# All engines issue in the written order, the softmax goes behind the rope, the cut one slot later

## The chip, the cores and the metric

The kernel runs on one core of a Trainium2 chip. Its time is the device time of one execution in microseconds (us), given as the median of several runs. The core's engines are TensorE (PE in the rows; its weight loads are PEld), VectorE (DVE), ScalarE (ACT), GpSimd (POOL) and SyncE (SP), which issues most of the DMAs. Each engine takes its instructions strictly in order: one that waits holds up all that stands behind it on that engine.

## What is computed

Two layers of a decoder over all 512 positions of one sequence, in float32. Both have 16 heads of 128, four key and value heads, and a gate beside the attention:

```
def dsa_mixer(h, w_in, q_g, k_g, w_out):
    q, k, v, gate, qi, ki, wi = split_cols(h @ w_in, A_WIDTHS)
    q = rope(rms_norm(q.reshape(B, T, N_HEADS, HEAD_DIM), q_g), pos)
    k = rope(rms_norm(k.reshape(B, T, N_KV_HEADS, HEAD_DIM), k_g), pos)
    ...
    logits = jnp.where(valid, jnp.einsum('bqgrd,bqkgd->bqgrk', qb, k_sel) * scale, NEG)
    p = jax.nn.softmax(logits, axis=-1)
    o = jnp.einsum('bqgrk,bqkgd->bqgrd', p, v_sel)
    return (jax.nn.silu(gate) * o) @ w_out

def moba_mixer(h, w_in, q_g, k_g, w_out):
    ...

h = h + dsa_mixer(rms_norm(h, a_norm[0]), ...)
h = h + moba_mixer(rms_norm(h, b_norm[0]), ...)
```

In the first layer an indexer keeps the 128 best keys of each query (the part left out in the middle); the second layer is the same without an indexer, with causal attention over blocks of 256 keys.

## The kernel before, in words

**Slots.** All projections are cut into tiles of 128 output columns over 2048 input rows, and each tile into four quarters. A quarter is a slot: `units` lists 484 of them in the order in which TensorE takes them. A weight quarter is loaded as `raw`, split two slots ahead into a high and a low part (`split`: `whi` cast on ACT, `wlo` subtracted on DVE), and multiplied in twelve 512-column matmuls, high by high, high by low and low by high (`products`, L193 to L195). The first 36 slots belong to layer 0's indexer. Then each layer has four groups of 40 slots: a k tile, a v tile, and four heads' q and gate tiles in the order q0 q1 g0 q2 g1 q3 g2 g3. Layer 0's output tiles begin at slot 196, layer 1 at 260, its output tiles at 420.

**A loop over slots** (the end of `build`) writes, for slot i: the split of slot i + 2, raw loads, the twelve matmuls, `maybe_attend`, and then the functions that were hung on this slot with `later(k, f)`, in the order in which they were hung; `later(k, f, True)` puts one at the front.

**A q tile** whose last slot is D hangs up s1 on D + 1 (square and its first bf16 part b0 on ACT, then the rope: four operations on DVE), s2 on D + 2 (the other two bf16 parts: sq minus b0 on DVE, b1 on ACT, b2 on DVE; then qh on ACT and ql on DVE) and the column sums on D + 3 (`sums`, cs, twelve small matmuls on TensorE that need b0, b1 and b2; one slot later for the first eight heads of layer 0). A k tile goes alike.

**A head's attention** begins with twelve score matmuls at a slot A (`attend`, L444 to L446) and hangs up the rest: `soft` on A + 1 (four masked maxima and four biases nb on DVE, four exponentials on ACT), `norm` on A + 2 (a reciprocal on DVE, four scalings on ACT), `turn` on A + 2 (four block transposes of 128x320 on DVE into u), `move` on A + 3 and A + 4 (16 DMAs from u to pt, which SP issues), `cuts` on A + 7 (pt is split into ph, cast on ACT, and pl, subtracted on DVE), `pv` on A + 9 (15 matmuls with the values on TensorE), and `gate` and `rest` on A + 10 and A + 11. Attends stand at least seven or eight slots apart (`maybe_attend`). In layer 1 they come at offsets 15, 23, 31 and 39 of a group's 40 slots (30 and 37 for the last two heads), so that `soft` of a group's first, second and third head falls into a slot that also holds the s1 of a q tile.

**What sets the order.** PE and SP issue in the written order throughout (`manual_schedule`, L106). ACT, DVE and POOL do so only for the first 46 slots (`OPENING`); behind them the framework's scheduler orders these three when the program is built. The orders in the section on the change show what it chose.

The lines of the call order:

```
for i in range(len(units)):
    ...
    split(i + SPLIT)
    ...
    load(i + SPLIT)
    ...
    products(i)
    maybe_attend(A if i < second else B)
    pending = hooks.get(i, [])
    while pending:
        pending.pop(0)()
```

Of the kernel before, what the change touches and what calls it, by code (L numbers as in the profile page):

```python
# [93 lines left out]
def build(tc, a):  # L94
    nc = tc.nc
    ctx = ExitStack()
# [6 lines left out]
    dp = pool("dram", space=DRAM)  # L103
    pp = pool("psum", space=PSUM)
    E = mybir.EngineType
    ctx.enter_context(tc.manual_schedule(engines={E.PE, E.SP}))  # L106
    opening = ExitStack()
    opening.enter_context(tc.manual_schedule(engines={E.Activation, E.DVE, E.Pool}))

    def t512(tag, name, dt=F32, bufs=None, p=None, cols=T):  # L110
        return (p or kp).tile([P, cols], dt, tag=tag, name=name, **({"bufs": bufs} if bufs else {}))
# [22 lines left out]
    def later(k, f, first=False):  # L134
        fs = hooks.setdefault(now[0] + k, [])
        fs.insert(0 if first else len(fs), f)
# [1 line left out]
    def at(slot, f):  # L138
        hooks.setdefault(slot, []).append(f)

    OPENING = 46
    SLOT, SPARE = 2.6, 0.5
    dve, gps = Paced(nc.vector, 1.05e-3), Paced(nc.gpsimd, 2.1e-3)

# [15 lines left out]
    def load(upto, most=99):  # L160

        while most and issued[0] < len(loads) and (issued[0] < RAW or loads[issued[0] - RAW][3] <= upto):
            t, q, m, _ = loads[issued[0]]
            raw = wp.tile([P, 4 * m, t.cols], F32, tag="raw", name=f"raw_{t.name}_{q}", bufs=RAW)
            src = t.src.rearrange("p (k n) -> p k n", n=t.cols)
            nc.sync.dma_start(raw, src[:, 4 * q:4 * (q + m)])
            for k in range(m):
                t.raw[q + k] = raw[:, 4 * k:4 * k + 4]
            issued[0] += 1
            most -= 1  # L170

    def split(i):
        if i >= len(units):
            return
        t, q = units[i]
        hi = wp.tile([P, 4, t.cols], F32R, tag="whi", name=f"whi_{t.name}_{q}", bufs=3)
        lo = wp.tile([P, 4, t.cols], F32R, tag="wlo", name=f"wlo_{t.name}_{q}", bufs=3)
        r = t.raw[q]
        nc.scalar.copy(hi, r)  # L179
        eng = gps if fill else dve  # L180
        eng.tensor_tensor(lo, r, hi.bitcast(F32), op=OP.subtract)
        t.cut[q] = (hi, lo)

    def products(i):
        t, q = units[i]
        if q == 0:
            t.z = ps("pj", f"z_{t.name}", 3)
        hi, lo = t.cut[q]
        o = t.z[:t.cols, :T - t.t0]
        for k in range(4):  # L190
            kt = 4 * q + k
            xh, xl = (x[:, t.t0:] for x in t.X[kt])
            nc.tensor.matmul(o, lhsT=hi[:, k], rhs=xh, start=kt == 0, stop=False)  # L193
            nc.tensor.matmul(o, lhsT=hi[:, k], rhs=xl, start=False, stop=False)  # L194
            nc.tensor.matmul(o, lhsT=lo[:, k], rhs=xh, start=False, stop=kt == KT - 1)  # L195
        if q == 3:
            t.done(t.z)
# [33 lines left out]
    def cut_hi(hi, src):  # L231
        nc.scalar.copy(hi, src)

    def cut_lo(lo, src, hi):
        dve.tensor_tensor(lo, src, hi.bitcast(F32), op=OP.subtract)
# [198 lines left out]
    def attend(Y, h):  # L434
# [43 lines left out]
        def move(js):  # L478
            for j in js:
                for i in range(4):  # L480
                    nc.sync.dma_start(v.t[BLK * j:BLK * j + BLK, 320 * i:320 * i + 320],  # L481
                                      v.u[BLK * i:BLK * i + BLK, 320 * j:320 * j + 320])

        def cuts(hi, lo):
            if 0 in hi:
                v.ph = t512("ph", f"ph{n}", F32R, cols=1280)
                v.pl = t512("pl", f"pl{n}", F32R, cols=1280)
            for i in hi:
                o = slice(640 * i, 640 * i + 640)
                cut_hi(v.ph[:, o], v.t[:, o])  # L490
            for i in lo:
                o = slice(640 * i, 640 * i + 640)
                cut_lo(v.pl[:, o], v.t[:, o], v.ph[:, o])
# [25 lines left out]
        def rest():  # L519
            cut_lo(Y.B[h][1], v.og, Y.B[h][0])  # L520

        later(1, soft, True)
        for k, f in ((2, norm), (2, turn), (3, lambda: move((0, 1))), (4, lambda: move((2, 3))),
                     (7, lambda: cuts((0, 1), (0, 1))), (9, pv), (10, gate), (11, rest)):
            later(k, f)

    def maybe_attend(Y):
        h = Y.head
        apart = 7 if h >= HEADS - 2 or (Y.L == 0 and h < 12) else 8
        if h < HEADS and Y.open and h in Y.qslot and now[0] >= Y.qslot[h] + 4 and now[0] >= Y.slot + apart:  # L530
            Y.head, Y.slot = h + 1, now[0]
            attend(Y, h)
# [258 lines left out]
    def load_x(q):  # L791
        for kt in range(4 * q, 4 * q + 4):
            nc.sync.dma_start(xs[kt], a["xT"][kt])

    def take_x(q):
        for kt in range(4 * q, 4 * q + 4):
            take(X0, kt, xs[kt], gains[:, kt:kt + 1], 0)
# [16 lines left out]
    split(1)  # L814
    for i in range(len(units)):
        now[0] = i
        if i == OPENING:
            opening.close()
        dve.slot(i * SLOT)
        gps.slot(i * SLOT)  # L820
        if i in (2, 4):
            take_x(i // 2 + 1)
        split(i + SPLIT)
        if i == 0:
            take_x(1)
        if i in (0, 1):
            load(i + SPLIT, 1)
            load_x(i + 2)
        load(i + SPLIT)
        if i == 1:  # L830
            for n, t in (("cosi", cosi), ("sini", sini), ("cos", cos), ("sin", sin)):
                nc.sync.dma_start(t, a[n])
# [5 lines that stand above are left out]
        while fill and dve.until < (i + 1) * SLOT - SPARE:  # L838
            fill.pop(0)()
# [56 lines left out]
```

## Time and profile before

| | |
|---|---|
| median of 3 runs | 1519.15 us (1518.68 to 1520.04) |
| profiled execution | 1520.94 us |
| its span in the profile | 1519.2 us |
| mean granted clock of TensorE | 0.991 |
| DVE busy | 912.1 us, 60% |
| ACT busy | 695.2 us, 46% |
| POOL busy | 146.6 us, 10% |
| DMA | 170.86 MB, 112 GB/s mean |

The profile is that of one execution, which took 1.8 us more than the median. The span runs from its first to its last instruction. Busy times are sums over the span; matmuls are pipelined, so that one of 512 columns is shown with 0.39 us though the next starts some 0.23 us behind it. Names of tiles are given without their numbers: `cs_q` is any q tile's column sums. L77 is the line of a helper through which most operations of DVE and POOL are written, so these are told apart by their tiles. What stands in square brackets behind a row is the engine's idle time just before it, and what ended it.

### The profile page before, as it was taken

The numbers are of one execution on the slowest core, as the hardware profiler recorded it, in microseconds if no ns is written. First come the engines' busy times: TensorE is split into PE (matmuls) and PEld (weight loads), VectorE is DVE, ScalarE is ACT, GpSimd is POOL, SyncE is SP. The second block draws the span as 40 slices with busy tenths as digits, with TensorE's granted clock in tenths as the row PEclk, the third lists the DMA queues.
The fourth block names the chain that finished last, engine by engine and source line by source line (L and its number), as shares of the span: only waits on it lengthen the run. The fifth ranks groups of instructions, "written<-read, shape, count | busy, mean of one in ns | idle before, by whom it ended". The sixth has DMA issues, their size and how long they took to land.

```text
span 1519.2 us, 20709 instructions
## 1 busy us (share of the span) xinstructions
PE 1488.3 (98%) x7348; PEld 1244.3 (82%) x7348; DVE 912.1 (60%) x1848; ACT 695.2 (46%) x1332; POOL 146.6 (10%) x128
## 2 busy tenths in 40 slices
PE   8999999999899999899999999999999999899999
PEld 6998888888787888788888888887888888788887
DVE  6898966666666665644344565667565657543322
ACT  6874334545454444533333444455444545432221
POOL 0433540000000000001111000000000000000000
PEclk9999999999999999999999999999999999999999
DMA  7332223333323323254443233332323332344442
GB/s 246 105 97 84 86 95 103 102 106 100 108 83 112 107 74 116 76 172 146 146 145 125 80 97 113 102 100 91 115 87 118 100 113 88 90 126 163 146 145 90
DMA packets 74215, 170.86 MB, mean 112 GB/s; under 512 B 13824, under 2 KB 30976, under 8 KB 74112
## 3 DMA queue, kind: packets, MB, share of 16 engines
q1 hardware_dynamic: 74112, 169.55, 35.4%
q8 instruction: 57, 0.93, 0.2%
q14 instruction: 46, 0.38, 0.1%
HBM read 140.13 MB, written 8.39 MB: 98 GB/s over the span
## 4 chain that ended last, share of the span: by engine, by line
PE 64%; DVE 4%; SPq 3%; ACT 2%; issue 2%; DMA 1%; DVEq 0%; ACTq 0%
PE z_o L193 8%; PE z_o L194 8%; PE z_o L195 8%; PE z_g L193 5%; PE z_q L193 5%; PE z_q L195 5%; PE z_q L194 5%; PE z_g L195 4%; PE z_g L194 4%; SPq L481 3%; PE o L508 2%; PE z_v L193 1%; PE z_v L195 1%; PE z_v L194 1%; PE z_k L193 1%
## 5 line engine op out<-in xcount | busy, mean ns | idle before, releaser
L193 PE MATMUL z_g<-xh,whi_g 128*128 128x512 f32 x512 | 206.6, 403 | 0.0
L195 PE MATMUL z_g<-xh,wlo_g 128*128 128x512 f32 x512 | 203.1, 397 | 3.2 <-DVE wlo_g L77 3.2
L193 PE MATMUL z_q<-xh,whi_q 128*128 128x512 f32 x512 | 202.6, 396 | 0.0
L194 PE MATMUL z_g<-xl,whi_g 128*128 128x512 f32 x512 | 202.5, 395 | 0.0
L195 PE MATMUL z_q<-xh,wlo_q 128*128 128x512 f32 x512 | 200.1, 391 | 0.0
L194 PE MATMUL z_q<-xl,whi_q 128*128 128x512 f32 x512 | 199.8, 390 | 0.0
L193 PE MATMUL z_o<-bh,whi_o 128*128 128x512 f32 x512 | 199.6, 390 | 0.0
L195 PE MATMUL z_o<-bh,wlo_o 128*128 128x512 f32 x512 | 199.4, 390 | 0.0
L194 PE MATMUL z_o<-bl,whi_o 128*128 128x512 f32 x512 | 199.4, 389 | 0.0
L77 DVE TENSOR_TENSOR wlo_o<-raw_o,whi_o 128x512 fp32r<-128x512 f32 x128 | 88.9, 694 | 159.8 <-ACT whi_o L179 159.8
L179 ACT CAST whi_o<-raw_o 128x512 fp32r<-128x512 f32 x128 | 79.7, 622 | 220.0 <-PE z_o L194 211.5
L179 ACT CAST whi_g<-raw_g 128x512 fp32r<-128x512 f32 x128 | 78.0, 616 | 113.6 <-PE z_q L194 73.6
L179 ACT CAST whi_q<-raw_q 128x512 fp32r<-128x512 f32 x128 | 78.6, 618 | 107.8 <-PE z_q L194 59.9
L195 PEld LDWEIGHTS z_g<-xh,wlo_g 128*128 128x128 f32 x512 | 97.9, 191 | 26.0 <-DVE wlo_g L77 4.5
L77 DVE TENSOR_TENSOR wlo_g<-raw_g,whi_g 128x512 fp32r<-128x512 f32 x112 | 76.5, 686 | 68.3 <-ACT whi_g L179 66.1
L193 PEld LDWEIGHTS z_g<-xh,whi_g 128*128 128x128 f32 x512 | 97.9, 191 | 19.6 <-ACT whi_g L179 1.1
L194 PEld LDWEIGHTS z_g<-xl,whi_g 128*128 128x128 f32 x512 | 98.2, 192 | 18.8
L195 PEld LDWEIGHTS z_q<-xh,wlo_q 128*128 128x128 f32 x512 | 96.2, 188 | 20.5
L195 PEld LDWEIGHTS z_o<-bh,wlo_o 128*128 128x128 f32 x512 | 96.2, 188 | 20.0
L193 PEld LDWEIGHTS z_o<-bh,whi_o 128*128 128x128 f32 x512 | 96.1, 188 | 19.9
L194 PEld LDWEIGHTS z_q<-xl,whi_q 128*128 128x128 f32 x512 | 96.6, 189 | 19.2
L194 PEld LDWEIGHTS z_o<-bl,whi_o 128*128 128x128 f32 x512 | 96.2, 188 | 19.6
(167 smaller groups left out, 2707.3 us busy)
## 6 DMA issues: line engine op xcount, KB each, us to landing
pt<-u SPq DMA_DIRECT2D x512, 40.0 KB, 1.9
raw_q<-w_a SPq DMA_DIRECT2D x32, 512.0 KB, 3.8
raw_g<-w_a SPq DMA_DIRECT2D x32, 512.0 KB, 3.9
raw_q<-w_b SPq DMA_DIRECT2D x32, 512.0 KB, 3.6
raw_g<-w_b SPq DMA_DIRECT2D x32, 512.0 KB, 3.8
raw_o<-w_ao SPq DMA_DIRECT2D x26, 512.0 KB, 3.5
raw_o<-w_bo SPq DMA_DIRECT2D x26, 512.0 KB, 3.6
raw_qi<-w_a SPq DMA_DIRECT2D x14, 512.0 KB, 3.9
```

What stands on the lines that cost most here:

```text
L77: return f(out, *args, **kw)
L179: nc.scalar.copy(hi, r)
L193: nc.tensor.matmul(o, lhsT=hi[:, k], rhs=xh, start=kt == 0, stop=False)
L194: nc.tensor.matmul(o, lhsT=hi[:, k], rhs=xl, start=False, stop=False)
L195: nc.tensor.matmul(o, lhsT=lo[:, k], rhs=xh, start=False, stop=kt == KT - 1)
L481: nc.sync.dma_start(v.t[BLK * j:BLK * j + BLK, 320 * i:320 * i + 320], v.u[BLK * i:BLK * i + BLK, 320 * j:320 * j + 320])
L508: nc.tensor.matmul(o[:, q], lhsT=l[:, kt * P:kt * P + P], rhs=r[:, t], start=m == 0 and c == 0, stop=m == 4 and c == 2)
```

## The change

`manual_schedule` now takes in all five engines for the whole program, and the 46-slot opening is dropped. `soft` is no longer put at the front of its slot's functions but behind those already there. `cuts` stands eight slots behind the scores, no longer seven.

```
-    ctx.enter_context(tc.manual_schedule(engines={E.PE, E.SP}))
-    opening = ExitStack()
-    opening.enter_context(tc.manual_schedule(engines={E.Activation, E.DVE, E.Pool}))
+    ctx.enter_context(tc.manual_schedule(engines={E.PE, E.SP, E.Activation, E.DVE, E.Pool}))
...
-    OPENING = 46
...
-        later(1, soft, True)
+        later(1, soft)
         for k, f in ((2, norm), (2, turn), (3, lambda: move((0, 1))), (4, lambda: move((2, 3))),
-                     (7, lambda: cuts((0, 1), (0, 1))), (9, pv), (10, gate), (11, rest)):
+                     (8, lambda: cuts((0, 1), (0, 1))), (9, pv), (10, gate), (11, rest)):
             later(k, f)
...
-        if i == OPENING:
-            opening.close()
```

The order of PE and of SP is the same, instruction for instruction. On POOL three operations of layer 1's causal mask move. ACT and DVE change in many places; three follow. A name such as `wlo_g1_4_2` is the low weights of layer 1, gate tile of head 4, quarter 2; `S1_4` and `nb1_4` are head 4's scores and bias; ISA rows are the masked maximum and the reading of its accumulator.

DVE in layer 1, the slot that holds head 4's `soft` and the rope of head 5's q tile. Before:

```order
L77 TENSOR_TENSOR wlo_g1_4_2_9477<-raw_g1_4_2_9342,whi_g1_4_2_9476 128x512
L77 ISA S1_4_9493,mx1_4_9495<-s0_1_4_9457,mask_93 128x512
L77 ISA mx1_4_9495 128x1
L77 SCALAR_TENSOR_TENSOR t1_q1_5_9515<-z_q1_5_9360,gains_79,cos_91 128x512
L77 SCALAR_TENSOR_TENSOR nb1_4_9496<-mx1_4_9495,sc_q1_4_9474 128x1
L77 ISA S1_4_9493,mx1_4_9495<-s1_1_4_9458,mask_93 128x384
```

and after:

```order
L77 TENSOR_TENSOR wlo_g1_4_2_9474<-raw_g1_4_2_9339,whi_g1_4_2_9473 128x512
L77 SCALAR_TENSOR_TENSOR t1_q1_5_9496<-z_q1_5_9357,gains_77,cos_89 128x512
L77 SCALAR_TENSOR_TENSOR t2_q1_5_9497<-z_q1_5_9357,gains_77,sin_90 64x512 x2
L77 TENSOR_TENSOR t1_q1_5_9496<-t1_q1_5_9496,t2_q1_5_9497 128x512
L77 ISA S1_4_9502,mx1_4_9504<-s0_1_4_9454,mask_91 128x512
L77 ISA mx1_4_9504 128x1
L77 SCALAR_TENSOR_TENSOR nb1_4_9505<-mx1_4_9504,sc_q1_4_9471 128x1
```

Before, the first maximum stood right behind the weights, the rope's four operations were spread between and behind the maxima. Now the whole rope stands in front of the first maximum.

DVE a dozen rows on, the slot with the second and third bf16 part of head 5's q tile and with the transposes of head 4. Before:

```order
L77 TENSOR_TENSOR sq_q1_5_9509<-sq_q1_5_9509,b0_q1_5_9511 128x512
L77 TENSOR_TENSOR t1_q1_5_9515<-t1_q1_5_9515,t2_q1_5_9516 128x512
L77 TENSOR_TENSOR wlo_g1_4_3_9522<-raw_g1_4_2_9342,whi_g1_4_3_9521 128x512
L77 TENSOR_TENSOR b2_q1_5_9513<-sq_q1_5_9509,b1_q1_5_9512 128x512
L77 TENSOR_TENSOR ql_q1_5_9543<-t1_q1_5_9515,qh_q1_5_9542 128x512
L77 RECIPROCAL ri1_4_9546<-sm1_4_9494 128x4
L77 TENSOR_TENSOR wlo_q1_6_0_9559<-raw_q1_6_0_9389,whi_q1_6_0_9558 128x512
L77 STREAM_TRANSPOSE u1_4_9552<-S1_4_9493 128x320 x4
```

and after:

```order
L77 TENSOR_TENSOR wlo_g1_4_3_9519<-raw_g1_4_2_9339,whi_g1_4_3_9518 128x512
L77 TENSOR_TENSOR sq_q1_5_9490<-sq_q1_5_9490,b0_q1_5_9492 128x512
L77 TENSOR_TENSOR b2_q1_5_9494<-sq_q1_5_9490,b1_q1_5_9493 128x512
L77 TENSOR_TENSOR ql_q1_5_9540<-t1_q1_5_9496,qh_q1_5_9539 128x512
L77 RECIPROCAL ri1_4_9543<-sm1_4_9503 128x4
L77 STREAM_TRANSPOSE u1_4_9549<-S1_4_9502 128x320 x4
L77 TENSOR_TENSOR wlo_q1_6_0_9556<-raw_q1_6_0_9386,whi_q1_6_0_9555 128x512
```

The weights wlo_q1_6_0 stood ahead of the four transposes and now stand behind them.

ACT in layer 0, the cast ph of head 5. Before:

```order
L179 CAST whi_k0_2_3_3809<-raw_k0_2_2_3616 128x512
L232 CAST ph0_5_3842<-pt0_5_3707 128x640 x2
L179 CAST whi_v0_2_0_3850<-raw_v0_2_0_3716 128x512
L460 ACTIVATE S0_6_3866,sm0_6_3867<-S0_6_3866,nb0_6_3869,sc_q0_6_3411 128x512
L460 ACTIVATE S0_6_3866,sm0_6_3867<-S0_6_3866,nb0_6_3869,sc_q0_6_3411 128x384
```

and after:

```order
L176 CAST whi_k0_2_3_3806<-raw_k0_2_2_3607 128x512
L176 CAST whi_v0_2_0_3841<-raw_v0_2_0_3713 128x512
L229 CAST ph0_5_3857<-pt0_5_3704 128x640 x2
L457 ACTIVATE S0_6_3863,sm0_6_3864<-S0_6_3863,nb0_6_3866,sc_q0_6_3392 128x512
L457 ACTIVATE S0_6_3863,sm0_6_3864<-S0_6_3863,nb0_6_3866,sc_q0_6_3392 128x384
```

Here ph moves one row down, behind the next slot's high weights. In layer 1 it stands between whi_g1_5_1 and whi_g1_5_2 (head 4) in both orders, so it doesn't move there.

## Rows read from the trace of the kernel before

**Rows 1.** The page's part 1: engine, busy us, share of the span, instructions.

```profile
PE 1488.3 (98%) x7348; PEld 1244.3 (82%) x7348; DVE 912.1 (60%) x1848; ACT 695.2 (46%) x1332; POOL 146.6 (10%) x128
```

**Rows 2.** Waits of TensorE over the whole span: us in total, times, longest us.

```profile
PE cs_q L298 <- ACT b_q L291: 9.5, 3, 3.7
PE cs_k L298 <- DVE b_k L77: 4.3, 1, 4.3
PE z_g L195 <- DVE wlo_g L77: 3.2, 3, 1.1
PE cs_q L298 <- DVE b_q L77: 3.1, 5, 1.0
```

**Rows 3.** Windows, the stretches behind the four big stalls: us, busy (x), PEclk, DMA share, GB/s.

```profile
1318.66:1325.05 6.39, 6.39 (x24) 5.06 (x25) 1.81 (x4) 0.62 (x1) 1.01 (x1) 0.50 0.26 63
sum 23.14, PE 22.95 PEld 18.27 DVE 6.07 ACT 1.84 POOL 4.34; mean PE 5.74 PEld 4.57 DVE 1.52 ACT 0.46 POOL 1.08
```

**Rows 4.** Waits of all engines: us in total, times, longest us.

```profile
ACT ph L232 <- DMA pt<-u: 90.1, 29, 5.9
```

**Rows 5.** Timeline of DVE, layer 1 from head 4's softmax: start us, us.

```profile
994.02 0.69 DVE L77 TENSOR_TENSOR wlo_g<-raw_g,whi_g 128x512 fp32r<-128x512 f32 x1 [2.52 <-ACT whi_g L179]
...
999.01 0.69 DVE L77 TENSOR_TENSOR sq_q<-sq_q,b_q 128x512 f32<-128x512 f32 x1
...
1000.82 0.69 DVE L77 TENSOR_TENSOR b_q<-sq_q,b_q 128x512 bf16<-128x512 f32 x1
...
1002.12 0.66 DVE L77 TENSOR_TENSOR wlo_q<-raw_q,whi_q 128x512 fp32r<-128x512 f32 x1
1004.24 1.69 DVE L77 STREAM_TRANSPOSE u<-S 128x320 f32<-128x320 f32 x4 [1.47 <-ACT S L467]
```

**Rows 6.** Timeline of DVE, a rope (layer 1) and a first maximum (layer 0).

```profile
853.53 0.75 DVE L77 SCALAR_TENSOR_TENSOR t_q<-z_q,gains,cos 128x512 f32<-128x512 f32 x1
854.29 1.52 DVE L77 SCALAR_TENSOR_TENSOR t_q<-z_q,gains,sin 64x512 f32<-64x512 f32 x2
...
368.46 0.68 DVE L77 CUSTOM_DVE_ANT_0 S<-s,mask 128x512 f32<-128x512 f32 x1
...
369.25 0.16 DVE L77 SCALAR_TENSOR_TENSOR nb<-mx,sc_q 128x1 f32<-128x1 f32 x1
```

**Rows 7.** Timeline of ACT, the same heads as rows 5.

```profile
996.09 0.82 ACT L460 ACTIVATE S<-S,nb,sc_q 128x512 f32<-128x512 f32 x1 [0.95 <-DVE nb L77]
...
998.84 0.60 ACT L179 CAST whi_g<-raw_g 128x512 fp32r<-128x512 f32 x1
...
1002.29 1.92 ACT L467 ACTIVATE S<-S,ri 128x512 f32<-128x512 f32 x4 [0.81 <-DVE ri L77]
```

**Rows 8.** Timeline of TensorE: sums, next tile's first matmul, two attends (layer 1).

```profile
1003.47 0.45 PE L298 MATMUL cs_q<-ones_bf,b_q 128*128 128x1 bf16 x12
...
1006.64 0.39 PE L193 MATMUL z_q<-xh,whi_q 128*128 128x512 f32 x1
...
1017.53 0.39 PE L444 MATMUL s<-kh_k,qh_q 128*128 128x512 f32 x1
...
1043.68 0.39 PE L444 MATMUL s<-kh_k,qh_q 128*128 128x512 f32 x1
```

**Rows 9.** Timelines of ACT and DVE, the loop from ph to ph (layer 1).

```profile
1018.65 1.36 ACT L232 CAST ph<-pt 128x640 fp32r<-128x640 f32 x2 [3.25 <-DMA pt<-u]
...
1019.41 1.56 DVE L77 TENSOR_TENSOR pl<-pt,ph 128x640 fp32r<-128x640 f32 x2 [3.29 <-ACT ph L232]
...
1031.57 1.69 DVE L77 STREAM_TRANSPOSE u<-S 128x320 f32<-128x320 f32 x4 [0.87 <-ACT S L467]
...
1045.88 1.36 ACT L232 CAST ph<-pt 128x640 fp32r<-128x640 f32 x2 [4.34 <-DMA pt<-u]
```

**Rows 10.** Timelines of ACT and DVE, layer 0, between heads 13 and 14.

```profile
605.52 1.36 ACT L232 CAST ph<-pt 128x640 fp32r<-128x640 f32 x2 [3.99 <-DMA pt<-u]
...
620.01 0.68 DVE L77 TENSOR_TENSOR b_q<-sq_q,b_q 128x512 bf16<-128x512 f32 x1
```

## The prediction

> **What bounds the kernel now.** I began with the page's busy times: TensorE is busy 1488.3 us of the 1519.2 [rows 1]. [...]
>
> The waits of TensorE come next [rows 2]. The column sums of a rotary tile (cs, L298) wait for its second bf16 part b1 (ACT, L291), 9.5 us in three waits, once for k's third part (4.3) and five times for q's b2 (3.1). That is 16.9 at four places: k's, and three where a wait for b1 (the longest 3.7, so 2.9 each for the other two) is followed by one of up to 1.0 for b2. Three slots of gates wait for their low weights (z_g on wlo_g), 3.2 us. Behind each of the four big stalls the granted clock falls to 0.50, for 23.14 us in sum [rows 3]; at half speed that costs 11.6. So the stalls that can be given back are worth 16.9 + 11.6 + 3.2 = 31.7 us of 1521.
>
> Then the waits of the other engines [rows 4]: ACT stands 90.1 us in 29 waits at ph, the first cast of a head's probabilities, waiting for the transfers of pt. Those transfers feed back on themselves. ACT and DVE go in order, so what stands behind ph and pl (the next head's softmax, then the transposes that start the next transfers) is late when ph is late. From head 5's ph to head 6's ph are 1045.88 − 1018.65 = 27.2 us [rows 9], while TensorE needs 1043.68 − 1017.53 = 26.15 from attend to attend [rows 8]. The loop is a little longer than TensorE's period, so heads drift later until a longer interval between attends lets them catch up.
>
> **The change part by part.** *The cut one slot later* costs nothing where the transfers are late anyway. In layer 1 ph already stood one row behind the next slot's high weights, and stays there (the sentence behind the third pair of orders). In layer 0 it falls behind one more 0.6 us cast, which ACT's wait of up to 5.9 at that place covers; without that cover it is 0.6 us on the loop.
>
> *The softmax behind the rope.* Before, the scheduler wove a head's four masked maxima through the rope of a later q tile. Now the rope goes first, then the maxima with each bias right behind its own. A rope is 0.76 + 1.55 + 0.60 = 2.9 us of DVE, and the first maximum with its bias 0.95 [rows 6]. The exponentials on ACT need all 2.75 us behind that first bias [rows 7], and on ACT the next weights and b1 stand behind them. Before, sums had 2.0 us to spare at a group's first head; 2.9 us more is not covered.
>
> *The transposes ahead of the next weights.* Before, wlo_q6_0 ran at 1002.12 while DVE waited for ACT's normalization; now the four transposes (1004.24 to 1005.93) stand in front of it [rows 5].
>
> First head of a group, from the row of wlo_g at 994.02 [rows 5]. DVE's 512-column operations start 0.60 apart (three from 999.01 to 1000.82). wlo to 994.6, rope to 997.5, first bias 998.45, exponentials to 1001.2, high weights 1001.8, wlo 1002.4, the subtraction of b0 1003.0, b1 1003.7, b2 1004.4. The sums come due at 1003.47 [rows 8]: **1.0 us** of stall. Then ql and the reciprocal to 1005.2, normalization 1.92 [rows 7] to 1007.1, transposes to 1008.8, wlo_q6_0 1009.5. The third matmul needs it at 1006.64 + 0.45 + the 1.0 of slip = 1008.1 [rows 8]: **1.4**. Sum 2.4.
>
> Second and third head, counted from ph. pl is done at 2.2 (0.76 after ph, two of 0.74) [rows 9], wlo 2.8, rope 5.7, first bias 6.7, exponentials 9.4, high weights 9.9, wlo 10.5, the gate's product 11.1, subtraction 11.8, b1 12.5, b2 13.2. ph of head 5 moves with the transposes, from 1018.65 by 2.9 to 1021.6; the sums come due one period after the others, 1003.47 + 26.15, plus 2.4, at 1032.0, that is 10.4 behind ph. Stall **2.9**. Then ql and reciprocal 13.9, normalization 15.9, transposes 17.5, wlo behind them: **1.4** again, 4.3 per head. From the transposes' end (1031.57 + 1.69) to ph are 1045.88 − 1033.26 = 12.6 [rows 9]: the loop becomes 30.1, against a period of 26.15. The two agree: TensorE slips 4.0 to 4.3 per head whether it stands still or runs at the lower clock, because what it loses in one way shortens the next wait. Hence I add no half clock here.
>
> Fourth head: 0.5 (the longer interval absorbs most). Head 14 comes seven slots behind 13 and its softmax had no rope ahead in either order; b2 came 15.2 behind ph (605.52 to 620.69) [rows 10], the late transposes make it 17.3. The stall goes from 3.7 + 1.0 to about 6.8, with 1.5 of half clock (half of the 3 us lost behind a stall now, since a longer wait is followed by less work that is due): 8.3, for 6.9 now (4.7 and 2.2).
>
> Layer 1: three groups of 2.4 + 4.3 + 4.3 + 0.5 = 11.5 are 34.5, the last 2.4 + 4.3 + 8.3 = 15.0, together 49.5. Before it had 3.2 at z_g, 0.4 at one cs, and 2.9 + 1.0 with 3.2 of half clock (half of 6.39) at head 14: 10.7. **+38.8.**
>
> Layer 0: heads 0 to 7 go at intervals of seven slots whose softmax mostly has no rope beside it, and there the plain order is better: heads 0 to 5 no longer drift as far as the longest wait at ph (5.9) [rows 4], and k2's stall of 4.3 with 3.0 of half clock becomes about 1.6. Against that, by the same chains: head 8 2.1 and head 12 2.4 as first heads, head 13 4.4 as a second one, head 14 8.3 and head 9 (cramped like it) 8.1. With k2 that is 26.9. Before, k2 had 7.3, head 9 6.6 (one of the 2.9 stalls with what followed it and its half clock) and head 14 6.9: 20.8. **+6.1.**
>
> Output tiles, the transition between the layers and the index part keep their order but for three mask operations on GpSimd, and have neither softmax nor transposes; I cost them at nothing. Sum: 1520.94 + 38.8 + 6.1 = 1565.8 for a profiled execution, which stands 1.8 above the median of the runs. **1564 us.**
>
> [...] In the rows a 512-column fp32 subtraction is 0.69 us long, yet the next starts 0.60 behind it [rows 5]. [...]
>
> **The rivals.** *Faster, 1488.* The feedback through ph breaks: if ph never waits in front of work that is due, the four stalls go with their half clock, −16.9 − 11.6 − 3.2 from 1520.94, less the 1.8: about 1488. For it: 90.1 us of ACT's time is spent waiting at ph. Against: ph keeps its row in layer 1, and the rope adds 2.9 to the loop. It decides if the loop from ph to ph comes below 26.15. [...]
>
> *No change, 1519.* Layer 0's gain at k2 (about 5.8) and others like it at head 14 balance the losses at the ropes; it needs the softmax to move by under 0.5 us instead of 2.9, as if the weave before had cost nearly what the rope does.
>
> *Slower still, 1590.* The 2.9 us stalls bring the lower clock as those of 2.9 before did [rows 2, 3], some 3 us each in eight places, and the slip doesn't give it back: +24. Against it stands the loop's 30.1.
>
> **How the numbers follow.** Slower by these chains 0.87 (of it 0.12 for the case near 1590), faster 0.09, no change 0.04. What a measurement of this kernel can tell from no change is about 0.2%, 3 us. The bounds come from the chain's error: 1.5 us less in each of 17 stages (bias and exponentials wholly beside the rope) is −25, about 1539; half clock behind each 2.9 us stall about 1590. Range **1536 to 1592**.
>
> **What the changed profile would show.** In layer 1 TensorE's waits for b1 and b2 at L298's place in all four groups (about 1 us at a group's first head, 3 at the second and third), waits of z_q for wlo_q of about 1.4 that the profile before doesn't have; transposes about 3 us later behind attend; the loop from ph to ph near 30 us; the stall at k2 near 1.6. If the loop is 27 or less, my chains are wrong; if the waits at ph vanish and no sums wait, the faster rival holds; if many more than four stretches show 0.50, the slowest does.

## The result and the profile after

The changed kernel takes 1588.86 us (median of 4 runs, 1587.28 to 1589.68) and the kernel before, run beside it, 1519.6: a ratio of 1.045 (95% interval 1.0432 to 1.0468), so 69 us slower. The forecast was 1564, in a range of 1536 to 1592.

The page of the changed kernel begins thus (span, then busy time, share and instructions of each engine):

```profile
span 1585.2 us, 20726 instructions
...
PE 1512.3 (95%) x7348; PEld 1254.9 (79%) x7348; DVE 934.6 (59%) x1848; ACT 689.7 (44%) x1332; POOL 145.8 (9%) x128
```

Against [rows 1] the span grew by 66.0 us. TensorE's idle time grew from 30.9 to 72.9, that is by 42.0, and its busy time by 24.0 for the same 7348 matmuls. The waits of TensorE, with totals, times and longest, say where it stands:

```profile
PE cs_q L295 <- ACT b_q L288: 32.5, 13, 5.5
PE cs_q L295 <- DVE b_q L77: 10.2, 19, 0.6
PE z_q L192 <- DVE wlo_q L77: 7.5, 8, 1.1
PE cs_k L295 <- ACT b_k L288: 4.6, 1, 4.6
PE tv_v L352 <- DVE t_k L77: 3.0, 1, 3.0
```

The sums wait for b1 in 13 places instead of 3, and for b2 in 19 instead of 5 [rows 2]; z_q's waits for low weights behind the transposes are new, eight of them at about 1 us. Twelve times the granted clock falls from 1.00 to 0.50 (half clock below), each time at a wait of TensorE of 1.2 to 5.5 us or just behind it. At 0.50 the 512-column matmuls of a slot start 0.43 us apart (eleven of z_v from 393.59 to 397.86), at 1.00 0.23 (263.02 to 263.92). The first two of these stretches and the sum (us; busy of PE, PEld, DVE, ACT, POOL; granted clock, DMA share, GB/s):

```profile
258.69:262.10 3.41, 3.07 (x10) 2.59 (x11) 2.20 (x5) 2.04 (x4) 0.00 (x0) 0.50 0.76 204
391.81:398.64 6.83, 6.09 (x24) 4.84 (x25) 1.97 (x4) 1.68 (x4) 1.01 (x1) 0.50 0.58 170
...
sum 58.02, PE 49.29 PEld 39.39 DVE 30.63 ACT 29.05 POOL 5.03; mean PE 4.11 PEld 3.28 DVE 2.55 ACT 2.42 POOL 0.42
```

Some begin within the stall, so the busy time in them is what compares: 49.3 us of PE at 0.50, 22.95 in the four of [rows 3]. By the two distances nearly half of the difference is lost by it, which I estimate at 13 us; the other 11 of the 24 I have not assigned.

The slot of head 4 in layer 1, on DVE. It answers to [rows 5]; wlo_g of the first row is the same instruction as the one at 994.02 there:

```profile
1030.61 0.69 DVE L77 TENSOR_TENSOR wlo_g<-raw_g,whi_g 128x512 fp32r<-128x512 f32 x1 [2.46 <-ACT whi_g L176]
1031.22 0.75 DVE L77 SCALAR_TENSOR_TENSOR t_q<-z_q,gains,cos 128x512 f32<-128x512 f32 x1
...
1034.14 0.68 DVE L77 CUSTOM_DVE_ANT_0 S<-s,mask 128x512 f32<-128x512 f32 x1
...
1038.34 0.69 DVE L77 TENSOR_TENSOR wlo_g<-raw_g,whi_g 128x512 fp32r<-128x512 f32 x1 [1.62 <-ACT whi_g L176]
1038.95 0.68 DVE L77 TENSOR_TENSOR sq_q<-sq_q,b_q 128x512 f32<-128x512 f32 x1
1040.32 0.69 DVE L77 TENSOR_TENSOR b_q<-sq_q,b_q 128x512 bf16<-128x512 f32 x1 [0.69 <-ACT b_q L288]
...
1041.53 0.17 DVE L77 RECIPROCAL ri<-sm 128x4 f32<-128x4 f32 x1
1043.75 1.69 DVE L77 STREAM_TRANSPOSE u<-S 128x320 f32<-128x320 f32 x4 [2.05 <-ACT S L464]
1045.37 1.25 DVE L77 TENSOR_TENSOR wlo_q<-raw_q,whi_q 128x512 fp32r<-128x512 f32 x2
```

The square brackets tell the story. DVE stands idle for 1.62 us for the next slot's high weights, then for 0.69 for b1, then for 2.05 for ACT's normalization. Behind the first of these waits stands sq minus b0, whose operands ACT had finished at 1031.73; it runs at 1038.95. The transposes end 14.8 us behind wlo_g, before it was 11.9 (994.02 to 1005.93).

The loop from head 4's ph to head 5's, and two attends of TensorE, answer to [rows 8, 9]:

```profile
1058.02 0.73 ACT L229 CAST ph<-pt 128x640 fp32r<-128x640 f32 x1 [3.46 <-DMA pt<-u]
...
1088.99 0.73 ACT L229 CAST ph<-pt 128x640 fp32r<-128x640 f32 x1 [4.18 <-DMA pt<-u]
...
1056.64 0.39 PE L441 MATMUL s<-kh_k,qh_q 128*128 128x512 f32 x1
...
1086.89 0.39 PE L441 MATMUL s<-kh_k,qh_q 128*128 128x512 f32 x1
```

The loop is 31.0 us (27.2 before) and TensorE's interval between the attends of heads 5 and 6, which answers to it, 30.25 (26.15 before). It slips by 4.1. (The prediction takes the casts at 1018.65 and 1045.88 for those of heads 5 and 6; they are those of heads 4 and 5. Its sums aren't touched by that.)

Stretch by stretch, from the timelines of TensorE (the first score matmul of each head), in us, with two kernels of the experiments beside (man_act and man_sq_ri):

| stretch | before | after | DVE and POOL scheduled | two operations moved |
|---|---|---|---|---|
| start to layer 0's first attend | 221.7 | 222.1 | 220.3 | 219.7 |
| layer 0, head 0 to head 8 | 195.0 | 204.8 | 188.2 | 191.9 |
| layer 0, head 8, to layer 1, head 0 | 446.9 | 463.0 | 449.1 | 452.2 |
| layer 1, head 0 to head 15 | 466.5 | 504.6 | 473.5 | 486.7 |
| layer 1, head 15, to the end | 189.1 | 190.7 | 190.0 | 189.1 |

### The profile page after: what moved, and what is told of

Read it like the earlier page. It is cut to its first block, busy times and chain, and to the rows that moved or that the text cites. A ratio compares the mean times of both kernels' runs of the same rounds, so it can differ in the third digit from the quotient of the medians.

```text
span 1585.2 us, 20726 instructions
## 1 busy us (share of the span) xinstructions
PE 1512.3 (95%) x7348; PEld 1254.9 (79%) x7348; DVE 934.6 (59%) x1848; ACT 689.7 (44%) x1332; POOL 145.8 (9%) x128
## 4 chain that ended last, share of the span: by engine, by line
PE 61%; DVE 13%; ACT 9%; SPq 8%; DMA 4%; issue 4%; POOL 0%; DVEq 0%; ACTq 0%; POOLq 0%
SPq L478 8%; PE z_o L190 7%; PE z_o L191 7%; PE z_o L192 7%; PE z_q L190 4%; PE z_q L191 4%; PE z_q L192 4%; ACT S L457 4%; PE z_g L190 4%; DVE t_q L77 3%; PE z_g L192 3%; PE z_g L191 3%; DMA pt<-u 2%; PE o L505 2%; DVE wlo_g L77 2%
## 5 line engine op out<-in xcount | busy, mean ns | idle before, releaser
L77 DVE TENSOR_TENSOR wlo_o<-raw_o,whi_o 128x512 fp32r<-128x512 f32 x128 | 98.6, 772 | 196.1 <-ACT whi_o L176 196.0
L190 PE MATMUL z_g<-xh,whi_g 128*128 128x512 f32 x512 | 210.8, 412 | 1.4 <-ACT whi_g L176 1.4
L192 PE MATMUL z_g<-xh,wlo_g 128*128 128x512 f32 x512 | 206.7, 404 | 1.6 <-DVE wlo_g L77 1.6
L191 PE MATMUL z_g<-xl,whi_g 128*128 128x512 f32 x512 | 206.3, 403 | 0.0
L77 DVE TENSOR_TENSOR wlo_q<-raw_q,whi_q 128x512 fp32r<-128x512 f32 x114 | 77.1, 684 | 79.6 <-ACT whi_q L176 77.0
L192 PEld LDWEIGHTS z_q<-xh,wlo_q 128*128 128x128 f32 x512 | 96.4, 188 | 32.3 <-DVE wlo_q L77 11.9
L457 ACT ACTIVATE S<-S,nb,sc_q 128x512 f32<-128x512 f32 (+3 forms) x128 | 82.3, 644 | 78.8 <-DVE nb L77 78.8
L190 PEld LDWEIGHTS z_q<-xh,whi_q 128*128 128x128 f32 x512 | 96.9, 189 | 21.1 <-ACT whi_q L176 2.7
```

The lines of the kernel that those rows point to most:

```text
L77: return f(out, *args, **kw)
L457: nc.scalar.activation(s, s, AF.Exp, bias=nb[:, c], scale=sc[:, c], accum_out=v.sm[:, c])
```

## The experiments

Twelve kernels were run. They first took the change apart by its three edits, then by engine, then by operation. Two theories stood at the beginning. Theory A: the loss comes from where the softmax and the cut are written. Theory B: it comes from giving up the scheduler's order, wherever these stand.

### The written order alone (man_only)

```
-        later(1, soft)
+        later(1, soft, True)
...
-                     (8, lambda: cuts((0, 1), (0, 1))), (9, pv), (10, gate), (11, rest)):
+                     (7, lambda: cuts((0, 1), (0, 1))), (9, pv), (10, gate), (11, rest)):
```

> The changed kernel with the softmax back at the front of its slot and the cut back at seven slots, so that the written order of ACT, DVE and POOL alone is left of the change. Theory A (the loss comes from where the softmax, the transposes and the cut are written): layer 1 loses about 1 us at a group's first head (weights behind the transposes) and 2 to 2.5 at the second and third, layer 0 about nothing; 1535 us, between 1525 and 1545. Theory B (the loss comes from giving up the scheduler's weave as such, wherever the softmax is written): most of the 69 us stay, 1570 us or more.

Measured: 1594.28 us, ratio 1.0479 (1.0464 to 1.0495). Theory A falls as it stands: with softmax and cut back in their places the whole loss stays. The rows of the same slot say why the softmax in front doesn't help (DVE, then ACT):

```profile
1037.60 0.75 DVE L77 SCALAR_TENSOR_TENSOR t_q<-z_q,gains,cos 128x512 f32<-128x512 f32 x1 [1.59 <-ACT sq_q L274]
```

```profile
1036.41 0.59 ACT L457 ACTIVATE S<-S,nb,sc_q 128x256 f32<-128x256 f32 x1
...
1036.99 0.58 ACT L274 ACTIVATE sq_q<-z_q 128x512 f32<-128x512 f32 x1
```

Written in front, the softmax takes the square of the q tile behind its exponentials on ACT, and the rope begins 0.03 us behind the square's end. Before, the two were apart: the square and b0 stood ahead of the exponentials on ACT while the maxima stood ahead of the rope on DVE. No order of whole functions gives that, since each function writes on several engines at once. So this kernel takes one delay away and puts another in, and doesn't say what the softmax's place is worth by itself (man_weave below does).

### The cut back at seven slots (man_soft)

```
-                     (8, lambda: cuts((0, 1), (0, 1))), (9, pv), (10, gate), (11, rest)):
+                     (7, lambda: cuts((0, 1), (0, 1))), (9, pv), (10, gate), (11, rest)):
```

> The changed kernel with the cut back at seven slots; the softmax stays behind the rope, the order stays the written one. Theory A with the later cut as the cause of layer 0's loss in heads 0 to 7: those heads win back 10 to 15 us and layer 1 stays within 3 us, 1573 us. The prediction's own step (the later cut costs nothing): within 3 us of 1588.

Measured: 1598.52 us, ratio 1.051 (1.0494 to 1.0526). Both expectations missed. In the written order the later cut doesn't cost, it gives back 9.7 us. ACT's waits at ph are 134.2 us in this kernel:

```profile
ACT ph L229 <- DMA pt<-u: 134.2, 30, 6.8
```

With the cut at eight they are 67.2, so what stands behind ph on ACT is held less at that place. Which of these operations makes the gain was not tested. Layer 1 takes 514.4 us from head 0 to head 15 here and 504.6 with the later cut.

### The softmax in front again, where a rope shares its slot (man_cut8)

```
-        later(1, soft)
+        later(1, soft, 12 <= h < HEADS - 2 or (Y.L == 1 and h < 12))
```

> The changed kernel with the softmax back at the front of its slot in layer 1's heads 0 to 13 and layer 0's heads 12 and 13, the places where a rope shares its slot and attends stand eight slots apart; the cut stays at eight. Theory A (the rope in front of the softmax makes layer 1's loop from ph to ph 30 us): the loop in layer 1 falls to 27.5 to 28.5, layer 1 wins back 15 to 20 us, 1570 us. Theory B: within 5 us of 1588.

Measured: 1586.78 us, ratio 1.0429 (1.0411 to 1.0446), overlapping with the changed kernel's interval. Moved as a whole, the softmax is worth 2 us at most; the loop in layer 1 stays at 31 us (30.8).

### The later cut in the scheduled kernel (sched_cut8)

```
-                     (7, lambda: cuts((0, 1), (0, 1))), (9, pv), (10, gate), (11, rest)):
+                     (8, lambda: cuts((0, 1), (0, 1))), (9, pv), (10, gate), (11, rest)):
```

> The kernel before with the cut at eight slots; the scheduler stays, the softmax stays in front. If the later cut costs by itself, as layer 0 of the changed kernel suggests (ph no longer waits for its transfers and begins up to 5 us behind their landing): 1525 to 1535. If the scheduler moves the cut back to where its data are (in layer 1 it already stood at the later place): within 3 us of 1519.

Measured: 1522.16 us, ratio 1.0009 (1.0000 to 1.0019). The scheduler puts ph where it had stood, or nearly: ACT's waits there are 96.8 us, 90.1 before, and the longest is 5.9 in both. The edit is worth nothing there.

### One engine at a time (man_dve, man_act)

man_dve keeps the written order on DVE alone (beside PE and SP), man_act on ACT alone:

```
-    ctx.enter_context(tc.manual_schedule(engines={E.PE, E.SP, E.Activation, E.DVE, E.Pool}))
+    ctx.enter_context(tc.manual_schedule(engines={E.PE, E.SP, E.DVE}))
```

```
-    ctx.enter_context(tc.manual_schedule(engines={E.PE, E.SP, E.Activation, E.DVE, E.Pool}))
+    ctx.enter_context(tc.manual_schedule(engines={E.PE, E.SP, E.Activation}))
```

> The changed kernel with ACT and POOL given back to the scheduler; DVE stays in the written order. The kernels with the softmax put back in front have shown that its place is not what costs; theory B says that it is the weave given up, and asks on which engine. If it is DVE's order (the rope, the maxima, the transposes ahead of weights that are ready): within 10 us of 1588. If it is ACT's: under 1550.

> The changed kernel with DVE and POOL given back to the scheduler; ACT stays in the written order. If DVE's order costs: under 1550. If ACT's order costs (exponentials ahead of b1, normalization behind qh): within 10 us of 1588.

Measured: man_dve 1565.14 us, 1.0299 (1.0281 to 1.0316); man_act 1524.62 us, 1.003 (1.0019 to 1.0041). It is DVE's order above all: given back to the scheduler together with POOL, it takes 64 of the 69 us with it, though softmax, cut and ACT stay as the change wrote them. (POOL alone was not tried; the change moves three of its operations.) ACT and POOL given back are worth 24 us, and 33 behind the opening, since that kernel's scheduled opening is itself slower by 9.4 (231.5 us to the first attend). The two sum to more than 69, so a part of the loss needs both orders. DVE's rows of man_act, the same slot, and at the end one of the next head's:

```profile
990.67 0.74 DVE L77 SCALAR_TENSOR_TENSOR t_q<-z_q,gains,cos 128x512 f32<-128x512 f32 x1
...
992.97 0.69 DVE L77 CUSTOM_DVE_ANT_0 S<-s,mask 128x512 f32<-128x512 f32 x1
...
995.44 0.69 DVE L77 TENSOR_TENSOR sq_q<-sq_q,b_q 128x512 f32<-128x512 f32 x1
996.04 0.15 DVE L77 SCALAR_TENSOR_TENSOR nb<-mx,sc_q 128x1 f32<-128x1 f32 x1
997.08 0.18 DVE L77 RECIPROCAL ri<-sm 128x4 f32<-128x4 f32 x1 [0.89 <-ACT S L457]
997.59 0.69 DVE L77 TENSOR_TENSOR wlo_g<-raw_g,whi_g 128x512 fp32r<-128x512 f32 x1 [0.33 <-ACT whi_g L176]
998.20 0.68 DVE L77 TENSOR_TENSOR b_q<-sq_q,b_q 128x512 bf16<-128x512 f32 x1
...
1000.45 1.69 DVE L77 STREAM_TRANSPOSE u<-S 128x320 f32<-128x320 f32 x4 [0.29 <-ACT S L464]
...
1022.97 0.69 DVE L77 SCALAR_TENSOR_TENSOR og<-o,gu_g 128x512 f32<-128x512 f32 x1
```

Even here most of the rope stands ahead of the maxima, so with the rest of DVE's order as it is here that costs little. Two other things are different from the changed kernel's rows: sq minus b0 runs among the biases, ahead of the wait for the weights, and the reciprocal stands ahead of the weights and b2. DVE's waits in this stretch are 0.89, 0.33 and 0.29 (and one of 0.52 at u_q) where they were 1.62, 0.69 and 2.05.

### Square, softmax, rope by hand (man_weave)

The kernel with the written order alone, and s1 cut in two, so that a slot's functions are square and b0, softmax, rope:

```
         def s1():
-            v.n = Norm(v.z, n)
             v.r = rope(v.z, Y.qg, n)
+        def s0():
+            v.n = Norm(v.z, n)
...
+            later(1, s0, True)
...
-        later(1, soft, True)
+        put_soft(soft)
...
```

`put_soft` hangs the softmax behind the s0 of its slot and ahead of all else.

> All engines in the written order, cut at seven slots, and in a slot that holds both the order is now square and b0, then the softmax, then the rope, so that neither the rope waits for the exponentials (through the square) nor the maxima for the rope. From the rows: b2 of a group's first head comes just in time, the loop from ph to ph is 28.4 us, 2.2 us of slip at the second and third head of layer 1. If that pair of waits is what the written order costs: 1570 us (1562 to 1578). If it is ready work held behind waits everywhere (weights behind transposes, a v tile behind them): within 6 us of the 1594 that the softmax in front of the square gave.

Measured: 1571.28 us, ratio 1.0334 (1.0319 to 1.035), as worked out from the rows in total, but partly by luck: the loop from head 4's ph to head 5's is 29.2 us, not 28.4, and TensorE slips 3.6 between heads 5 and 6, not 2.2. The coupling through the square was worth 23 of man_only's 74 us. Against man_soft, where the softmax stands behind square and rope and the cut is at seven too, this kernel gains 27 us. So the rope in front of the softmax does cost, where the square is not pushed back for it. (The s0 goes to the front of its slot for every q tile, also ahead of other functions; that part was not taken apart.)

### The sums one slot later (sums4)

```
-            for k, f in ((1, s1), (2, s2), (3 + early, s2b), (4 + early, s3)):
+            for k, f in ((1, s1), (2, s2), (4 if h % GROUP else 3 + early, s2b), (5 if h % GROUP else 4 + early, s3)):
```

> The changed kernel with the column sums of heads 1 to 3 of each group one slot (2.7 us) later, where TensorE now waits for b1 and b2. If the wait at the sums is itself the loss: first and second heads lose nothing there, third heads about 4 us, 1562 us. If TensorE slips because the loop from ph to ph is longer than its period, wherever it waits: the stall shows up elsewhere and the time stays within 6 us of 1588.

Measured: 1582.3 us, ratio 1.0407 (1.0387 to 1.0427), at the edge of the second expectation. The waits at q's sums (32.5 and 10.2) are gone from the list, and others have grown in their place:

```profile
PE z_q L190 <- ACT whi_q L176: 13.2, 11, 2.8
PE z_q L192 <- DVE wlo_q L77: 11.9, 13, 1.1
PE z_g L192 <- DVE wlo_g L77: 10.2, 11, 1.7
PE o L505 <- ACT ph L229: 5.7, 2, 3.1
...
PE z_g L190 <- ACT whi_g L176: 4.2, 4, 1.5
```

These lines hold 45.2 us, in the changed kernel the same five hold 12.2: 33 of the 43 us have moved to the weights and the values. TensorE follows the loop from ph to ph, not the place where it happens to wait.

### Two operations moved by hand (man_sq, man_sq_ri)

In man_sq the first operation of `middle` stands at the end of slot D + 1; in man_sq_ri the reciprocal of `norm` also stands at the end of its softmax's slot. Everything else is the changed kernel, all engines in the written order. `end` hangs a function behind all others of a slot:

```
+            end(1, lambda: v.n.first())
             for k, f in ((1, s1), (2, s2), (3 + early, s2b), (4 + early, s3)):
...
         later(1, soft)
+        end(1, recip)
```

> The changed kernel, all engines in the written order, with one operation per rotary tile moved by hand to where the scheduler had put it: sq minus b0 stands at the end of slot D + 1, ahead of the next slot's low weights instead of behind them (with its engine it waits there for the high weights, which stand behind the exponentials). If the loss is ready work queued behind that wait: b1, b2 and the transposes come 1.4 us earlier, the slip at the second and third head of layer 1 falls from 4.1 to 2.7, 1568 us. If the place of the weights and transposes is what costs: within 6 us of 1588.

> As the kernel with sq minus b0 moved, and the reciprocal of the softmax also moved up, to the end of its softmax's slot, so that ACT's normalization no longer waits behind b2 and ql of DVE. By the rows 0.8 us earlier transposes on top: slip 1.9 per head, 1558 us. If the reciprocal's place is of no account: within 4 us of the kernel with sq alone.

Measured: man_sq 1572.05 us, 1.0342 (1.0326 to 1.0358); man_sq_ri 1542.69 us, 1.0146 (1.0133 to 1.016). One 0.6 us operation per tile moved by one place is worth 17 us, one of 0.17 us per head another 29, nearly three times the 10 that I expected of it. The first total was nearly met, but not by the mechanism: TensorE's slip between heads 5 and 6 of layer 1, which was to fall from 4.1 to 2.7 and then to 1.9, is 4.4 and 4.0, and of the 17 us layer 1 has 5.0, heads 0 to 7 of layer 0 have 5.3. Of the 29, layer 1 has 12.9, and 16.2 lie between layer 0's first attend and layer 1's. DVE in man_sq_ri, the same slot:

```profile
999.83 0.69 DVE L77 TENSOR_TENSOR wlo_g<-raw_g,whi_g 128x512 fp32r<-128x512 f32 x1 [2.41 <-ACT whi_g L181]
...
1005.85 0.69 DVE L77 TENSOR_TENSOR sq_q<-sq_q,b_q 128x512 f32<-128x512 f32 x1
...
1007.05 0.18 DVE L77 RECIPROCAL ri<-sm 128x4 f32<-128x4 f32 x1 [0.51 <-ACT S L466]
1007.56 0.69 DVE L77 TENSOR_TENSOR wlo_g<-raw_g,whi_g 128x512 fp32r<-128x512 f32 x1 [0.33 <-ACT whi_g L181]
1008.17 0.68 DVE L77 TENSOR_TENSOR b_q<-sq_q,b_q 128x512 bf16<-128x512 f32 x1
...
1010.43 1.70 DVE L77 STREAM_TRANSPOSE u<-S 128x320 f32<-128x320 f32 x4 [0.97 <-ACT S L476]
1012.04 1.25 DVE L77 TENSOR_TENSOR wlo_q<-raw_q,whi_q 128x512 fp32r<-128x512 f32 x2
```

From the first wlo_g to the end of the transposes it is now 12.3 us; 14.8 in the changed kernel, 11.9 before. With this z_q's waits for wlo_q fall from 7.5 to 0.4 us, though the transposes still stand ahead of these weights: they are simply early enough. The reciprocal's new place is not the scheduler's in this slot: in the kernel before it stands behind b2 and ql too (second pair of orders). There its move makes up for other delays. In heads 0 to 7 of layer 0 it does give back what was lost (see below).

### A version that beats both (sums_before, sums_before_k)

The edit of sums4 made to the kernel before, and the same with k's sums a slot later:

```
-            for k, f in ((1, s1), (2, s2), (3, s2b), (4, s3), (5, s4), (6, s5), (7, s6)):
+            for k, f in ((1, s1), (2, s2), (4, s2b), (4, s3), (5, s4), (6, s5), (7, s6)):
```

> The kernel before (scheduler and all) with the column sums of heads 1 to 3 of each group one slot later: three of its four big stalls are waits at those sums. If these stalls are losses by themselves: 9.5 + 3 of waits and 8.6 of half clock go, 1498 to 1503 us. If they are what the loop from ph to ph takes from TensorE's period, they come back as waits for weights: 1512 us or more.

> As the kernel before with later q sums, and the k tiles' sums one slot later too (k of the third group in layer 0 has a wait of 4.3 us and 3 us of half clock there): another 4 to 7 us under the kernel with later q sums alone, if that stall is its own; the same time if it only moves.

Measured: sums_before 1509.44 us, 0.9926 (0.9913 to 0.9938); sums_before_k 1509.61 us, 0.9928 (0.9916 to 0.9941). The first is 11 us faster than the kernel before, between its two expectations: about half of the 21 that the three stalls cost, with their half clock, was their own. Part of the rest is seen in other waits: z_g's for weights rose from 3.2 [rows 2] to 6.7 us, and 1.6 came at the values' matmuls. k's stall only moves: it goes from cs_k to the v tile's transposes behind it.

```profile
PE tv_v L355 <- DVE t_k L77: 4.0, 2, 3.0
```

## Why the prediction was right, and where it was not

**Direction, and the chain in layer 1, hold.** TensorE's matmul order is the same and the loss is at the sums, with new waits of z_q for wlo_q, as forecast. Layer 1 was worked out at +38.8 us and measured at +38.1. The first head's chain stands in the rows: b2 was to begin 9.7 us behind wlo_g and does (1030.61 to 1040.32), the transposes were to end at 14.8 and do. The loop was to be 30.1 us and is 31.0; TensorE slips 2.5 at a group's first head (1029.95 to 1056.64, 24.17 before), forecast 2.4, and 4.1 between heads 5 and 6 (30.25 for 26.15), within the prediction's 4.0 to 4.3. The waits themselves are shorter in the profile than worked out (0.55 for 1.0 at the first head's sums, 1.68 and 0.55 for 2.9 at the second's); it is the slips that agree. sums4 shows that this slip is the loop's and not the sums': taken from there, most of the waits come back at the weights. That is also why half clock needed no term of its own in layer 1: between heads 9 and 10 (1197.03 to 1227.60) no stretch shows it, and TensorE slips 4.4 there, as much as where it does.

**The term that was mis-sized is layer 0, heads 0 to 7.** The prediction had these win 5.7 us (k2's stall from 7.3 to 1.6), on the ground that the plain order is better where no rope shares the softmax's slot. They lost 9.8. k2's stall is 4.6 + 0.5, with 3.0 lost at half clock (half of the 6.09 us busy at 391.81), and the v tile's transposes wait 3.0, with 1.5 at half clock (258.69), where I had left them at 1.0. That is 10 of the 15.5 us between forecast and result; most of the rest are slips of 1.3 to 1.7 us between heads 2 and 3, 5 and 6, 7 and 8.

The step that failed is that only softmax slots with a rope suffer. In these eight heads the reciprocal stands behind the next slot's low weights, not behind b2 and ql. It begins 1.15 to 2.35 us behind the last exponential; before, and in man_sq_ri, it began 0.03 behind. With sq minus b0 moved these heads take 199.5 us, with the reciprocal too 191.9, less than the 195.0 before. So 3.1 of the 5.7 us that I forecast are there once these two are out of the way.

A second delay was in no chain of mine for layer 0: the `gate` of an earlier head stands ahead of a tile's s1. The slot of k2's square, first DVE, then ACT:

```profile
379.61 0.69 DVE L77 TENSOR_TENSOR wlo_v<-raw_v,whi_v 128x512 fp32r<-128x512 f32 x1 [1.69 <-ACT whi_v L176]
380.22 0.17 DVE L77 RECIPROCAL ri<-sm 128x4 f32<-128x4 f32 x1
382.44 1.69 DVE L77 STREAM_TRANSPOSE u<-S 128x320 f32<-128x320 f32 x4 [2.05 <-ACT S L464]
...
386.49 0.75 DVE L77 SCALAR_TENSOR_TENSOR t_k<-z_k,gains,cos 128x512 f32<-128x512 f32 x1 [1.19 <-ACT sq_k L274]
```

```profile
385.34 0.62 ACT L229 CAST bh<-og 128x512 fp32r<-128x512 f32 x1 [2.42 <-DVE og L77]
385.87 0.59 ACT L274 ACTIVATE sq_k<-z_k 128x512 f32<-128x512 f32 x1
```

DVE's og stands behind the transposes, ACT's bh waits 2.42 us for it with the square behind itself, and the rope then waits 1.19 for the square. No run takes this delay out by itself.

**The rest of layer 0** was +11.8 and came out at +16.1. A tile between heads 10 and 11, for which I had no term, is 4.1 of that, nearly the whole difference: its sums wait 1.95 + 0.55 us, with 3.4 us at half clock behind them. Its bh waits for og and its rope for the square as k2's do, by 2.42 and 1.18.

**The softmax behind the rope is a part of the cause, not the whole of it.** The chain's length was read correctly from the new order, but taking the softmax back in front as a whole (man_only against man_soft, man_cut8 against the changed kernel) gains 2 to 4 us, since the square then goes behind the exponentials. With the square kept ahead of it, it gains 27 (man_weave against man_soft, both with the cut at seven), and 51 us of loss still remain. Those come in the main from ready operations that stand behind waits, on DVE above all (man_act); with two of these moved, 46 of the 69 us go though the softmax stays behind the rope.

**The later cut at nothing** holds for the scheduled kernel (ratio 1.0009) and fails for the written order, where it is a gain of 9.7 us; the sum didn't need that, since it was made for the three edits together.

**The rivals.** The one of no change falls with the 69 us: the first maximum begins 3.5 us behind wlo_g, 0.6 before, so the softmax moved by the rope's 2.9 and not by under 0.5. The faster one is refuted: the waits at ph fell from 90.1 to 67.2 us and the loop grew. The one near 1590 gives almost the measured time, but by another way than it said: half clock did rise (twelve stretches instead of four), yet in layer 1 it added nothing to the slip; the excess lies in layer 0.

**The distance of 0.60** holds in the changed kernel: wlo_g is 0.69 us long and the next operation begins 0.61 behind its start (1038.34 to 1038.95).

What stays open: of man_sq_ri's remaining 22 us over the kernel before, layer 1 has 20, 15 of them at the second head of each group; the first heads lose nothing. Its cause was not tried. The rows of head 5 there, ACT and then DVE, show a candidate:

```profile
1036.19 0.62 ACT L234 CAST bh<-og 128x512 fp32r<-128x512 f32 x1 [1.36 <-DVE og L77]
1036.71 0.61 ACT L295 CAST b_q<-sq_q 128x512 bf16<-128x512 f32 x1
...
1037.36 0.69 DVE L77 TENSOR_TENSOR b_q<-sq_q,b_q 128x512 bf16<-128x512 f32 x1 [1.20 <-ACT b_q L295]
```

b1 stands behind the gate's bh, which waits for an og that DVE has behind the weights. In man_act DVE's og stands ahead of them, right behind the biases (1022.97 in its rows). Moving the transposes behind the next weights, or ACT's order beside DVE's, are other candidates.

## What to carry to other kernels

When an engine issues in order, look not at how much work it has (DVE is 60% busy here) but for its short waits, and at what stands ready behind each of them: here a 0.17 us reciprocal per head, moved ahead of such a wait, gave 29 us, since it starts the chain that leads to the next transfers. A function that writes on three engines at once can't be put in the right place by moving the function; split it by engine or operation. A kernel in which two delays trade places says nothing of either; test the one with the other held. And where a stall sits on a loop that is longer than the bounding engine's period, taking the stall away moves it, or most of it (33 of 43 us in sums4): shorten the loop first.

## What was not expected of the hardware

The rope's first operation, on DVE, began 0.03 us behind the end of ACT's square, though both only read the tile's sums z (1036.99 + 0.58 and 1037.60 in the written order alone). Neither needs the other's result. The kernel before has it too:

```profile
612.51 0.75 DVE L77 SCALAR_TENSOR_TENSOR t_q<-z_q,gains,cos 128x512 f32<-128x512 f32 x1 [0.30 <-ACT sq_q L277]
```

Over the 40 q and k tiles of the kernel before, and over those of the changed one, the shortest distance from the square's end to the rope is 0.03 us. In the code z is the only tile that both touch, so it is probably the reading of z that the wait guards; no run separates that from other causes.
